# Earlier token sums, a written order for the last part's first pair and norm, and operands on multiples of 512 bytes, in a one-core trunk layer

## The chip, the cores and the metric

The kernel runs on one core of a Trainium2 chip. The metric is the device time of one execution in microseconds (us). Five engines have queues of their own: TensorE (PE, matmuls), VectorE (DVE), ScalarE (ACT), GpSimd (POOL) and SyncE (SP, which only issues transfers here; POOL issues some too).

## The reference, cut to what matters

The reference is one decoder layer for 512 tokens of width 1024. The change touches its two feed-forward parts and nothing of the mixer's arithmetic.

```python
D_MODEL, SEQ, D_FF = 1024, 512, 2816

def rmsnorm(x, g):
    y = x * lax.rsqrt(jnp.mean(x * x, axis=-1, keepdims=True) + EPS)
    return y * g

def swiglu(x, w_in, w_out):
    a, b = jnp.split(x @ w_in, 2, axis=-1)
    return (jax.nn.silu(a) * b) @ w_out

h = x + 0.5 * swiglu(rmsnorm(x, ffn1_norm), ffn1_w_in, ffn1_w_out)
h = h + hybrid_mixer(rmsnorm(h, mix_norm), w_in, ...)   # projection, HGRN2, gated delta rule, output
h = h + 0.5 * swiglu(rmsnorm(h, ffn2_norm), ffn2_w_in, ffn2_w_out)
y = rmsnorm(h, final_norm)
```

## The kernel before, in words

**Data.** Features lie on the 128 partitions and the 512 tokens along the free axis, so the stream `h` is 8 tiles of 128x512. Every float32 product is made of three matmuls: both operands are split into a high part (a rounded copy) and a low part (the rest), and high·high, high·low and low·high are summed in PSUM (`mm3`, lines 166 to 168). For the weights the names are `whi` and `wlo`, for the normalised tokens `uh` and `ul`. The stationary operand is a 128x128 piece of the weights; the tokens stream past it, 512 or 256 columns at a time.

**A feed-forward part** has two stages. The first makes `silu(a)·b` in 22 pieces of 128 hidden columns. A few pieces are computed plainly: the opening (lines 597 to 657) computes three of the first part's, and `ffn` (line 239) one of the second part's. The other 19 or 21 run by Strassen's scheme with seven products in place of eight (`product`, line 388): A11, A12 and A22 use weights as they come (`plain`, lines 343 to 361), s1 to s4 use sums of weight blocks (`sigma`, lines 362 to 386: three sums on DVE, a high part `sig` on ACT, a low part on DVE), and four of the products need sums of tokens, t1 to t4. These are made once, in place in `h` (`tokens`, lines 281 to 302): eight scalings on ACT (L284), four sums on DVE (L287 to L293) and their split in four halves, `th` on ACT (L299) and `tl` on DVE (L301). Each product is 12 matmuls of 256 columns, so a piece is 84. Its results are collected by `columns` (copies of PSUM, of which L433 is the first one of a piece) and `gate` (L465 to L473: scale by the norm, Silu, multiply into `g`). The plain pieces go through `first` (L488 to L494) instead. The second stage multiplies by the second matrix: the first four of eight output tiles are woven between the pieces (`first_half`, `down`), the rest follows in `ffn`.

**Low parts of plain weights.** `plain` writes the negative high part into the `wlo` tile on ACT (L349) and the high part into `whi` (L352); POOL then issues a transfer that adds the weights from memory to `wlo` (L358). In all other places DVE subtracts.

**What sets the order.** Within `gated` nothing is scheduled by a compiler: `Desk` (line 50) runs these functions as threads at build time with hand-set costs and lags, and the order it finds on each engine is written out (`manual_schedule`). The opening is written out by hand the same way. The rest of the program, the mixer and the second part's plain pieces and norm among it, is placed by a scheduler. Tiles come from rings: 3 `raw` buffers of 128x512 for loads, 2 `raw2` of twice the size, 6 each of `whi` and `wlo`; PSUM lanes `mm` (2 banks), `a` and `b` (2 each). A lane's `get` waits until all that held it is read.

**The norm** of a part needs the sum of squares of all tokens: `sqacc` squares each tile of `h` (ACT) and adds it to `acc` (POOL, in the opening DVE); `stats` (line 206) sums over partitions with eight tiny matmuls `pst`, takes the root on POOL (`root`, `rcol`, L225), spreads it with `pbc` matmuls and copies it to `rbc`. The products of the first stage do not need it; `gate` and `first` do.

## Time and profile before

| | us |
|---|---|
| median of 3 runs | 1649.01 (1648.87 to 1649.12) |
| the profiled execution | 1648.81 |
| its span | 1647.0 |
| PE busy in the span | 1609.5 (98%) |
| DVE, ACT, POOL busy | 1132.4, 857.9, 414.0 |
| first part: last plain matmul of the opening starts, first piece's first L433 copy | 42.67, 46.99 |
| second part: norm's `pbc` starts, first piece's first L433 copy | 1281.31, 1292.59 |

The time of an execution is its span and 1.8 us around it. All moments below are counted from the span's start. PE's busy time includes matmuls that run back to back at whatever clock they get, so a busy share of 98% does not say that they run at full rate; the views by window give the granted clock (PEclk, 1.00 is full speed) beside it. In a row of the timeline stand the start, the duration, the engine and the line, the operation, out<-in with sizes, and in brackets the idle time of the engine just before and what ended it.

### The profile page before, as it was taken

How to read it: one execution, taken by the hardware profiler on the slowest of the kernel's cores; microseconds unless marked ns; L12 is line 12 of the kernel's file. 1: busy time of each engine (PE TensorE's matmuls, PEld its weight loads, DVE VectorE, ACT ScalarE, POOL GpSimd, SP SyncE). 2: the span in 40 equal slices, each digit the busy share in tenths (PEclk: the TensorE clock that was granted, in tenths of full speed). 3: DMA queues.
4: the chain of work that ended last, by engine and by line, in shares of the span. 5: the costliest groups of instructions: out<-in, count | busy, mean ns of one | idle time of the engine just before them, and what ended most of it. 6: DMA issues, size and time to landing. Idle time of an engine off the chain costs nothing.

```text
span 1647.0 us, 30275 instructions
## 1 busy us (share of the span) xinstructions
PE 1609.5 (98%) x11178; PEld 1414.3 (86%) x11178; DVE 1132.4 (69%) x2158; ACT 857.9 (52%) x1852; POOL 414.0 (25%) x743
## 2 busy tenths in 40 slices
PE   8799999999999999999999999999999699999997
PEld 7799998888878788888888988887888699999887
DVE  5877775547677678658888888755544677778353
ACT  6666664323424335456666665554225666667232
POOL 1222210101121221253572655500001222220011
PEclk9999999999999999999999999999999799999999
DMA  5888852532312223443333333445534788883343
GB/s 179 194 185 183 186 122 80 176 115 91 93 50 72 84 72 96 126 144 103 100 100 113 92 104 121 144 146 181 185 103 154 180 186 181 184 184 87 109 137 116
DMA packets 128166, 216.53 MB, mean 131 GB/s; under 512 B 21888, under 2 KB 27776, under 8 KB 128016
## 3 DMA queue, kind: packets, MB, share of 16 engines
q1 hardware_dynamic: 110448, 182.89, 35.4%
q0 software_dynamic: 17280, 31.46, 12.7%
q8 instruction: 88, 1.44, 0.4%
q14 instruction: 62, 0.51, 0.1%
q10 hardware_dynamic: 288, 0.22, 0.0%
HBM read 197.45 MB, written 17.07 MB: 130 GB/s over the span
## 4 chain that ended last, share of the span: by engine, by line
PE 94%; issue 2%; DMA 1%; DVE 1%; ACT 1%; POOL 0%; DVEq 0%; SPq 0%; POOLq 0%
PE pmm L166 16%; PE pmm L168 16%; PE pmm L167 15%; PE pnat L166 4%; PE pfa L168 4%; PE pnat L168 4%; PE pnat L167 4%; PE pfa L166 4%; PE pfa L167 4%; PE pfy L168 2%; PE pfy L166 2%; PE pfy L167 2%; PE pfx L168 2%; PE pfx L167 2%; PE pfx L166 2%
## 5 line engine op out<-in xcount | busy, mean ns | idle before, releaser
L166 PE MATMUL pmm<-uh,whi 128*128 128x512 f32 x632 | 263.9, 418 | 5.4 <-ACT whi L623 5.4
L1766 ACT CAST whi<-raw 128x512 fp32r<-128x512 f32 x226 | 140.1, 620 | 215.7 <-PE pmm L167 156.2
L1768 DVE TENSOR_TENSOR wlo<-raw,whi 128x512 fp32r<-128x512 f32 x226 | 161.1, 715 | 126.7 <-ACT whi L1766 120.7
L168 PE MATMUL pmm<-uh,wlo 128*128 128x512 f32 x632 | 248.1, 393 | 0.0
L167 PE MATMUL pmm<-ul,whi 128*128 128x512 f32 x632 | 247.7, 392 | 0.0
L383 DVE TENSOR_TENSOR sig<-h,sig 128x1024 fp32r<-128x1024 f32 x80 | 97.7, 1221 | 76.8 <-ACT sig L381 76.7
L166 PEld LDWEIGHTS pmm<-uh,whi 128*128 128x128 f32 x632 | 119.5, 189 | 27.0 <-ACT whi L623 5.4
L166 PE MATMUL pmm<-gh,whi 128*128 128x512 f32 (+1 forms) x374 | 142.0, 380 | 0.0
L168 PE MATMUL pmm<-gh,wlo 128*128 128x512 f32 (+1 forms) x374 | 142.0, 380 | 0.0
L167 PE MATMUL pmm<-gl,whi 128*128 128x512 f32 (+1 forms) x374 | 141.9, 379 | 0.0
L168 PEld LDWEIGHTS pmm<-uh,wlo 128*128 128x128 f32 x632 | 119.0, 188 | 26.3
L167 PEld LDWEIGHTS pmm<-ul,whi 128*128 128x128 f32 x632 | 119.6, 189 | 20.4 <-DVE ul L193 0.2
L381 ACT CAST sig<-h 128x1024 fp32r<-128x1024 f32 x80 | 83.9, 1049 | 100.5 <-PE pfa L168 91.3
L204 POOL TENSOR_TENSOR acc<-acc,sqt 128x512 f32<-128x512 f32 x18 | 24.0, 1334 | 379.6 <-ACT sqt L202 294.5
L162 DVE TENSOR_TENSOR wlo<-raw,whi 128x512 fp32r<-128x512 f32 x78 | 59.2, 762 | 74.5 <-ACT whi L161 74.5
L166 PE MATMUL pnat<-whi,uh 128*128 128x256 f32 (+1 forms) x328 | 107.7, 328 | 0.0
L168 PE MATMUL pnat<-whi,ul 128*128 128x256 f32 (+1 forms) x328 | 100.6, 307 | 0.0
L167 PE MATMUL pnat<-wlo,uh 128*128 128x256 f32 (+1 forms) x328 | 100.4, 306 | 0.0
L166 PE MATMUL pfa<-th,sig 128*128 128x256 f32 x320 | 92.2, 288 | 5.0 <-ACT sig L381 5.0
L168 PE MATMUL pfa<-th,sig 128*128 128x256 f32 x320 | 92.3, 288 | 3.2 <-DVE sig L383 3.2
L358 POOL DMA_DIRECT2D wlo<-w1b x63 | 54.6, 869 | 157.5 <-ACT s L433 99.6
L161 ACT CAST whi<-raw 128x512 fp32r<-128x512 f32 x78 | 46.3, 595 | 87.5 <-PE pmm L167 81.1
(480 smaller groups left out, 4613.8 us busy)
## 6 DMA issues: line engine op xcount, KB each, us to landing
raw<-wt SPq DMA_DIRECT2D x128, 256.0 KB
raw<-w1b SPq DMA_DIRECT2D x88, 256.0 KB
raw<-w1a SPq DMA_DIRECT2D x80, 256.0 KB
raw<-wn SPq DMA_DIRECT2D x64, 256.0 KB
wlo<-w1b POOLq DMA_DIRECT2D x63, 256.0 KB, 5.3
wlo<-w1a POOLq DMA_DIRECT2D x57, 256.0 KB, 5.5
raw<-w2b SPq DMA_DIRECT2D x45, 256.0 KB
raw<-w2a SPq DMA_DIRECT2D x40, 256.0 KB
```

The lines of the kernel that those rows point to most:

```text
L161: act.copy(hi[:, :f], raw[:, :f])
L162: dve.tensor_tensor(lo[:, :f], raw[:, :f], hi[:, :f].bitcast(F32), op=ALU.subtract)
L166: pe.matmul(pt, ah, bh, start=first, stop=False, **kw)
L167: pe.matmul(pt, ah, bl, start=False, stop=False, **kw)
L168: pe.matmul(pt, al, bh, start=False, stop=last, **kw)
L204: add.tensor_tensor(acc, acc, s, op=ALU.add)
L358: pool.dma_start(lo, src_, accum_op=ALU.add)
L381: act.copy(hl[:, 0:2], s)
L383: dve.tensor_tensor(hl[:, 2:4], s, hl[:, 0:2].bitcast(F32), op=ALU.subtract)
L1766: act.copy(hi, raw)
L1768: dve.tensor_tensor(lo, raw, hi.bitcast(F32), op=ALU.subtract)
```

## The change

Five things are done.

1. **The opening** scales each token tile right after its square, makes the token sums (now eight of 128x2x256, `sums`) and their split (`high`, `low`, class `tokens`), all before the first gates. Its third plain pair is summed in the PSUM lane `b`, not in `mm`.
2. **The first pieces** of both parts get other lags in `plain`, `sigma` and `first`, and so another order.
3. **The second part's** plain piece and norm (`plain_pairs`, `norm`) become threads of the planner. The last square is added to `acc` by POOL, so that `pst` is four matmuls.
4. **Silu** is called once on one column ahead of the second part's sums, so that its table of values is loaded; the scheduler, not the planner, has placed this call.
5. **Sizes.** `msq` becomes 128x128 and all rings of the part are laid out beforehand (`room`). Before, `g`, `gh`, `gl`, `raw2`, `th`, `tl` and `sig` of the first part began 32 bytes behind a multiple of 512 in each partition, and those of the second part at multiples of 512; now all begin at multiples of 512.

```diff
-    v = pl.tile([P, 4], F32, name="msq", bufs=1)
+    v = pl.tile([P, P], F32, name="msq", bufs=1)
...
-        early, ahead = [], []
+        early, tk = [], tokens(fp)
+        fp.tile([P, P], F32, tag="msq", name="room", bufs=1)
+        for tag, n, size in (("fa", 2, 1), ("fb", 2, 1), ("s14", 2, 1), ("s23", 2, 1), ("raw2", 2, 2), ("g", KF + 2, 1), ("big", 7, 4)):
+            fp.tile([P, size * T], F32, tag=tag, name="room", bufs=n)
         if lead is not None:
-            early, ahead = opening(w1, fp)
-            early = early + ahead
+            early = opening(w1, fp, tk)
             lead()
-        else:
-            for j in range(late):
-                for n in ("fa", "fb"):
-                    early.append(fp.tile([P, T], F32, name=n, bufs=2))
-                    act.copy(early[-1], dense(w1[j, len(early) % 2 ^ 1], KD, ux))
-        g, gh = gated(w1, w2, src, after, fp, early, lead is not None)
+        g, gh = gated(w1, w2, src, after, fp, early, tk, late)
...
+class tokens:
+
+
+
+    def __init__(self, fp):
+        self.fp, self.hq = fp, h.rearrange("p (x a) t -> p x a t", x=2)
+        self.th, self.tl = [None] * 2, [None] * 2
+
+    def scale(self, kt, c0):
+        act.activation(h[:, kt], h[:, kt], AF.Copy, scale=cs[:, c0 + kt:c0 + kt + 1])
+
+    def sums(self, g):
+        a, lo, hi = slice(2 * g, 2 * g + 2), slice(0, T // 2), slice(T // 2, T)
+        b11, b12, b21, b22 = (self.hq[:, x, a, c] for x in range(2) for c in (lo, hi))
+        yield dve.tensor_tensor(b11, b11, b12, op=ALU.subtract)
+        yield dve.tensor_tensor(b12, b22, b12, op=ALU.subtract)
+        yield dve.scalar_tensor_tensor(b22, b11, -1.0, b22, op0=ALU.mult, op1=ALU.subtract)
+        yield dve.scalar_tensor_tensor(b21, b22, -1.0, b21, op0=ALU.mult, op1=ALU.subtract)
+
+    def high(self, g, x):
+        if g == 0:
+            self.th[x], self.tl[x] = (self.fp.tile([P, 4, T], F32R, tag="big", name=n, bufs=7) for n in ("th", "tl"))
+        a = slice(2 * g, 2 * g + 2)
+        act.copy(self.th[x][:, a], self.hq[:, x, a])
+
+    def low(self, g, x):
+        a = slice(2 * g, 2 * g + 2)
+        dve.tensor_tensor(self.tl[x][:, a], self.hq[:, x, a], self.th[x][:, a].bitcast(F32), op=ALU.subtract)
...
+    opened = bool(early)
+    n0 = len(early) // 2 if opened else late
+    D = Desk(raw=RB, w=WB, raw2=2, sig=3, sum=2, fa=2, fb=2, s14=2, s23=2, mm=2, a=0 if opened else 2,
+             b=0 if opened else 2)
...
-    def tokens():
-        for kt in range(KD):
-            yield A(T)
-            act.activation(h[:, kt], h[:, kt], AF.Copy, scale=cs[:, D.c0 + kt:D.c0 + kt + 1])
...
+    def sums_of_tokens():
+        if not opened:
+            act.activation(rcols[:, 4:5], ones[:, :1], AF.Silu)
+            for kt in (0, 1, 4, 5, 2, 3, 6, 7):
+                if kt == 2:
+                    yield "lag", 2.0
+                yield A(T) if kt == 7 else ("use", "ACT", 0.02)
+                tk.scale(kt, C_F2)
+            for g in range(2):
+                for step in range(4):
+                    yield V(T) if g else ("use", "DVE", 0.02)
+                    if step == 0:
+                        it = tk.sums(g)
+                    next(it)
+                D.start((0, g), splits(g))
+            yield "on", ("split", 0), ("split", 1)
+        D.fire("tokens")
+
+    def splits(g):
         for x in range(2):
...
+            yield A(2 * T)
+            tk.high(g, x)
+            yield V(2 * T)
+            tk.low(g, x)
+        D.fire(("split", g))
...
     def loader():
+        if not opened:
+            for j in range(n0):
+                for n in range(4):
+                    yield "get", "raw", 1
+                    raw = wp.tile([P, T], F32, tag="raw", name="raw", bufs=RB)
+                    yield S
+                    sp.dma_start(raw, w1[j, n // 2, :, n % 2 * T:n % 2 * T + T])
+                    D.start((-1, j, n), split_slab(("late", j, n), raw, T))
...
-        yield "lag", 3.0
+        yield "lag", 0.0 if j == n0 else 3.0
...
     def sigma(j, r2, r12, r21):
-        yield "lag", 3.0
+        yield "lag", (0.0, 8.0 if opened else 5.0, 4.0, 3.0)[min(j - n0, 3)]
...
     def first(j):
-        a, b = early[2 * j:2 * j + 2]
-        if not opened or j == 0:
-            yield from gate(j, a, b, -1.0, a)
+        if not opened:
+            yield "on", "tokens", "rbc", ("early", 4 * j + 1)
+        a = early[2 * j]
+        if opened and j == 0:
+            yield "lag", 6.0
+            yield from gate(j, a, early[1], -1.0, a)
             return
-        tag = "a" if j == 1 else "mm"
+        tags = ("a" if j == 1 else "b",) * 2 if opened else ("mm", "a")
+        yield "lag", (0.0 if j == 1 else 7.0) if opened else 6.0
...
         t = fp.tile([P, T], F32, name="fa", bufs=2)
         dve.tensor_tensor(t, a, rbc, op=ALU.mult)
-        D.put(tag)
+        D.put(tags[0])
...
+        if not opened:
+            yield "on", ("early", 4 * j + 3)
...
-        dve.scalar_tensor_tensor(g[j], b, -1.0, t, op0=ALU.mult, op1=ALU.mult)
-        D.put(tag)
+        dve.scalar_tensor_tensor(g[j], early[2 * j + 1], -1.0, t, op0=ALU.mult, op1=ALU.mult)
+        D.put(tags[1])
...
+    def plain_pairs():
+        for j in range(0 if opened else n0):
+            for n in range(4):
+                yield "on", ("late", j, n)
+                if n % 2 == 0:
+                    yield "get", "a" if n else "mm", 1
+                hi, lo = made["late", j, n]
+                for i in range(4):
+                    yield T_(.69)
+                    if n % 2 == 0 and i == 0:
+                        early.append(psc.tile([P, T], F32, tag="pa", name="pmm", bufs=LANES["a"]) if n else
+                                     psd.tile([P, T], F32, tag="mm", name="pmm"))
+                    w = slice(i * P, (i + 1) * P)
+                    mm3(early[-1], hi[:, w], lo[:, w], *ux(n % 2 * 4 + i), n % 2 == 0 and i == 0, n % 2 == 1 and i == 3)
+                D.put("w")
+                D.fire(("early", 4 * j + n))
+
+    def norm():
+        yield "lag", 6.0
+        yield T_(.95)
+        pt = psc.tile([P, T], F32, tag="pd", name="pst")
+        for i in range(NT):
+            pe.matmul(pt[:, i:i + 1], acc[:, i * P:(i + 1) * P], ones[:, :1], start=True, stop=True)
+        yield V(4)
+        v = fp.tile([P, P], F32, name="msq", bufs=1)
+        dve.tensor_scalar(v[:, :4], pt[:, :4], 1.0 / (P * KD), EPS, op0=ALU.mult, op1=ALU.add)
+        yield "use", "POOL", 1.3
+        pool.tensor_tensor(rcol, v[:, :4], mhalf[:, :4], op=ALU.pow)
+        yield "lag", 4.0
+        yield T_(.5)
+        pb = psc.tile([P, T], F32, tag="pd", name="pbc")
+        for i in range(NT):
+            pe.matmul(pb[:, i * P:(i + 1) * P], rcol[:, i:i + 1].to_broadcast([P, P]), ident, start=True, stop=True)
+        yield A(T)
+        act.copy(rbc, pb)
+        D.fire("rbc")
...
+        yield from plain_pairs()
         yield from product()
...
+    if opened:
+        D.idle.update(PE=8.0, DVE=3.0)
+    else:
+        D.start((0, 9), norm())
+    D.start((0,), sums_of_tokens())
...
+        if d == KD - 1 and (defer or late):
             act.activation(rbc, h[:, d], AF.Square)
+            if late:
+                pool.tensor_tensor(acc, acc, rbc, op=ALU.add)
             return
...
                 sqacc(kt - 1, pl, tag="s14", add=dve)
+                tk.scale(kt - 1, C_F1)
         s = sqacc(KD - 1, pl, tag="s14")
+        tk.scale(KD - 1, C_F1)
         slabs = [slab(w[2, 0][:, :512])]
+        for n in range(2):
+            for _ in tk.sums(n):
+                pass
+        tk.high(0, 0)
+        tk.high(0, 1)
         out = []
         for pt, n in zip(pts, ("fa", "fb")):
             out.append(pl.tile([P, T], F32, name=n, bufs=2))
             act.copy(out[-1], pt)
-        slabs.append(slab(w[2, 0][:, 512:]))
+        tk.high(1, 0)
+        tk.high(1, 1)
         more = []
         def half(n):
             if n % 2 == 0:
-                more.append(psd.tile([P, T], F32, tag="mm", name="pmm"))
+                more.append(psc.tile([P, T], F32, tag="pb", name="pmm", bufs=LANES["b"]))
             for i in range(4):
                 k, c = n % 2 * 4 + i, slice(i * P, (i + 1) * P)
                 mm3(more[-1], *(x[:, c] for x in slabs[n]), *ux(k), k == 0, k == KD - 1)
         def between():
+            slabs.append(slab(w[2, 0][:, 512:]))
             half(0)
+            tk.low(0, 0)
+            tk.low(0, 1)
             slabs.append(slab(w[2, 1][:, :512]))
+            tk.low(1, 0)
+            tk.low(1, 1)
         stats(pl, s, between)
         half(1)
         slabs.append(slab(w[2, 1][:, 512:]))
         half(2)
         half(3)
-    return out + pts[2:], more
+    return out + pts[2:] + more
...
-    e["nextnorm"](C_F2, e["h2"], tag="ta", bufs=TA)(d, mp)
+    e["nextnorm"](C_F2, e["h2"], late=True, tag="ta", bufs=TA)(d, mp)
```

VectorE between the opening and the first pieces, before (names: `wlo` of L162 is the low part of a slab of the third plain pair, `h` the token sums, `fa` and `g` gates):

```order
L162 TENSOR_TENSOR wlo<-raw,whi 128x512 x2
L224 TENSOR_SCALAR msq<-pst 128x4
L162 TENSOR_TENSOR wlo<-raw,whi 128x512
L465 TENSOR_TENSOR fa<-fa,rbc 128x512
L287 TENSOR_TENSOR h<-h 128x4x256
L162 TENSOR_TENSOR wlo<-raw,whi 128x512
L289 TENSOR_TENSOR h<-h 128x4x256
L291 SCALAR_TENSOR_TENSOR h<-h 128x4x256
L293 SCALAR_TENSOR_TENSOR h<-h 128x4x256
L473 SCALAR_TENSOR_TENSOR g<-fb,fa 128x512
L488 TENSOR_TENSOR fa<-pmm,rbc 128x512
L301 TENSOR_TENSOR tl<-h,th 128x1024
```

and now:

```order
L162 TENSOR_TENSOR wlo<-raw,whi 128x512
L264 TENSOR_TENSOR h<-h 128x2x256
L265 TENSOR_TENSOR h<-h 128x2x256
L266 SCALAR_TENSOR_TENSOR h<-h 128x2x256
L267 SCALAR_TENSOR_TENSOR h<-h 128x2x256
L264 TENSOR_TENSOR h<-h 128x2x256
L265 TENSOR_TENSOR h<-h 128x2x256
L266 SCALAR_TENSOR_TENSOR h<-h 128x2x256
L267 SCALAR_TENSOR_TENSOR h<-h 128x2x256
L224 TENSOR_SCALAR msq<-pst 128x4
L162 TENSOR_TENSOR wlo<-raw,whi 128x512
L277 TENSOR_TENSOR tl<-h,th 128x1024 x2
```

The sums have moved from behind the norm and the first gate to the place right behind the first slab, and the first `tl` ahead of all gates.

TensorE where the last slab of the third plain pair meets A11, the first product (`pfa`), in the changed kernel (before, all of the pair's 48 matmuls stood ahead of the first `pfa`):

```order
L166 MATMUL pmm_397<-uh_71,whi_392 128x512
L167 MATMUL pmm_397<-ul_72,whi_392 128x512
L168 MATMUL pfa_481<-uh_71,wlo_431 128x256
L166 MATMUL pfa_481<-uh_71,whi_430 128x256
L167 MATMUL pfa_481<-ul_72,whi_430 128x256
L168 MATMUL pfa_481<-uh_71,wlo_431 128x256
```

Most of A11's matmuls now run ahead of the last slab's; `whi_392` is the last slab's high part.

ScalarE where the second part begins, before (`fa` and `fb` are copies of the plain pair, `wlo` and `whi` of L349 and L352 belong to A11):

```order
L192 ACTIVATE uh<-h,cs 128x512
L202 ACTIVATE sqt<-h 128x512
L284 ACTIVATE h<-h,cs 128x512
L239 COPY fa<-pmm 128x512
L239 COPY fb<-pmm 128x512
L219 COPY rbc<-pbc 128x512
L467 ACT_TABLE_LOAD
L467 ACTIVATE fa<-fa 128x512
```

and now:

```order
L192 ACTIVATE uh<-h,cs 128x512
L674 ACTIVATE rbc<-h 128x512
L259 ACTIVATE h<-h,cs 128x512
L386 ACTIVATE wlo<-raw_14560 128x512
L273 CAST th<-h 128x1024
L389 CAST whi<-raw_14560 128x512
L386 ACTIVATE wlo<-raw 128x512
L273 CAST th<-h 128x1024
```

The weights of A11 and the token split follow the last scaling at once; the copies of the pair, which stood between, are gone, and `rbc` and the gate come later.

48 lines of the change are left out of this document (12 added, 36 removed).

## The prediction

> **What bounds the kernel now.** I read the page's busy times and its chain of waits first.
>
> ```profile
> span 1647.0 us, 30275 instructions
> PE 1609.5 (98%) x11178; PEld 1414.3 (86%) x11178; DVE 1132.4 (69%) x2158; ACT 857.9 (52%) x1852; POOL 414.0 (25%) x743
> PE 94%; issue 2%; DMA 1%; DVE 1%; ACT 1%; POOL 0%; DVEq 0%; SPq 0%; POOLq 0%
> ```
>
> The chain that ends last is PE for 94%. An edit helps only where PE stands still, runs at a low clock, or needs longer per matmul. The windows show where that is not so: PE busy, its granted clock (seventh figure) and DMA share.
>
> ```profile
> 100.00:240.00 140.00, 140.00 (x1174) 140.00 (x1173) 107.97 (x141) 92.45 (x162) 32.09 (x38) 1.00 0.77 169
> 1340.00:1480.00 140.00, 140.00 (x1169) 140.00 (x1168) 108.12 (x139) 96.08 (x168) 36.39 (x42) 1.00 0.82 184
> 1290.00:1300.00 10.00, 7.42 (x34) 6.60 (x34) 6.70 (x7) 5.31 (x9) 1.73 (x2) 0.67 0.74 123
> 1300.00:1310.00 10.00, 6.95 (x31) 6.65 (x32) 8.50 (x10) 6.01 (x9) 2.16 (x3) 0.50 0.87 255
> ```
>
> In the steady stretches of both feed-forward parts PE is full at clock 1.00. At the second part's start it is 70% busy at clock 0.67 and 0.50. The longest waits of PE around the two starts (total, times, longest; windows 0 to 62 and 1262 to 1312):
>
> ```profile
> PE pfa L166 <- ACT sig L381: 2.8, 1, 2.8
> PE pfa L166 <- DVE fa L488: 2.2, 1, 2.2
> PE pfy L167 <- DVE tl L301: 1.8, 2, 0.9
> PE pfa L168 <- DVE sig L383: 1.6, 1, 1.6
> ...
> PE pfa L166 <- ACT whi L352: 3.6, 1, 3.6
> PE pfa L168 <- DMA wlo<-w1b: 3.3, 1, 3.3
> PE pfa L166 <- ACT sig L381: 2.2, 1, 2.2
> PE pfa L168 <- DVE sig L383: 1.7, 1, 1.7
> ```
>
> Every one concerns what the change moves. But the waits (8.4 and 10.8 us) leave out what the lowered clock costs. So I measure by the beat: the first copy L433 of each piece, the first, third and fourth of either part.
>
> ```profile
> 46.99 0.37 ACT L433 COPY s<-pfa 128x256 f32<-128x256 f32 x1 [1.01 <-PE pfa L168]
> ...
> 76.75 0.35 ACT L433 COPY s<-pfa 128x256 f32<-128x256 f32 x1
> 86.78 0.35 ACT L433 COPY s<-pfa 128x256 f32<-128x256 f32 x1
> 1292.59 0.37 ACT L433 COPY s<-pfa 128x256 f32<-128x256 f32 x1 [1.10 <-PE pfa L168]
> ...
> 1324.40 0.35 ACT L433 COPY s<-pfa 128x256 f32<-128x256 f32 x1
> 1334.48 0.35 ACT L433 COPY s<-pfa 128x256 f32<-128x256 f32 x1
> ```
>
> The steady beat is 86.78 − 76.75 = 10.03 us and 1334.48 − 1324.40 = 10.08. Where the third copy could be is set by the last plain work on PE:
>
> ```profile
> 42.67 0.39 PE L168 MATMUL pmm<-uh,wlo 128*128 128x512 f32 x1
> 45.28 0.35 PE L166 MATMUL pfa<-uh,whi 128*128 128x256 f32 x1 [2.23 <-DVE fa L488]
> 1281.31 1.05 PE L217 MATMUL pbc<-sq,rcol 128*128 128x128 f32 x8
> 1286.00 0.54 PE L166 MATMUL pfa<-uh,whi 128*128 128x256 f32 x1 [3.65 <-ACT whi L352]
> ```
>
> In the first part the pair ends at 42.67 + 0.23 (the spacing of its matmuls) = 42.90. The copy follows the start of A11 by 46.99 − 45.28 = 1.71 us. Without a stall the third copy is at 42.90 + 1.71 + 2 × 10.03 = 64.67, and it is at 76.75: **12.1 us lost**. In the second part `pbc` takes until about 1282.24 (0.93 at the spacing of its eight), the third copy could be at 1282.24 + 1.71 + 20.16 = 1304.1, and is at 1324.40: **20.3 us lost**. That is what earlier operands can win.
>
> **The change part by part.** *The opening's sums.* Eight sums of 512 columns cost as much as `h<-h,raw` of that size, 0.69 to 0.72 apart:
>
> ```profile
> 52.72 0.69 DVE L371 TENSOR_TENSOR h<-h,raw 128x512 f32<-128x512 f32 x1
> 29.22 0.69 DVE L162 TENSOR_TENSOR wlo<-raw,whi 128x512 fp32r<-128x512 f32 x1 [5.72 <-ACT whi L161]
> ```
>
> 8 × 0.72 = 5.8 us fall on 5.72 us in which DVE waited anyway; the slab behind ends some 2.7 us later than before, at 32.65, and PE wants it after the `pst`, at 34.6 (half(1)). The four `tl` (4.9 us, 1.23 each by the L368 row of that size further down) then end at 37.9, before the first gate. On ACT the eight scalings and four `th` fill its idle time of 3.39 and 5.19 before 34.9. Cover for all of this is the third plain pair, 48 matmuls; without it the sums' 5.8 us would be PE's.
>
> *A11 and the first sums.* With the pair in lane `b`, A11 need not wait for `fa` (2.23 gone). Its bound is now its own low part. POOL issues that after ACT's `wlo`:
>
> ```profile
> 37.72 2.92 POOL L358 DMA_DIRECT2D wlo<-w1a  x3 [4.96 <-PE pmm L168]
> wlo<-w1a POOLq DMA_DIRECT2D x57, 256.0 KB, 5.5
> ```
>
> ACT writes it one Silu earlier, so the issue moves to about 36.8, and with 4.3 to 5.5 us to landing (the fastest I saw and the page's median) the tile is there at 41.1 to 42.3. The third matmul of A11 now stands ten 512-column matmuls before the pair's end: 42.90 − 10 × 0.23 + 2 × 0.12 = 40.8. The wait is 0.3 to 1.5, I take 0.8. Sums of weights: `sigma`'s three sums, `sig` and its low part come to 46.9 by DVE's new row; s2 wants them at 47.7. s1's may be up to 0.3 late; I take 0.2. First part: 12.1 − 1.0 = **11.1** (9.5 to 11.8).
>
> *The second part's start.* Here A11's first load waited behind the norm: its `raw2` lies where the pool of the part before had its root.
>
> ```profile
> 1269.51 0.32 SPq L586 DMA_DIRECT2D h<-h  x1
> 1277.90 0.33 SPq L316 DMA_DIRECT2D raw<-w1b  x1
> 1277.91 0.59 ACT L239 COPY fa<-pmm 128x512 f32<-128x512 f32 x1 [5.57 <-POOL rcol L225]
> ```
>
> The new order has no root ahead: SP issues at about 1269.9, 8 us sooner, and passes one spill row; that spill is read much later. ACT writes A11's parts instead of standing 5.57 us for `rcol`. POOL first adds the last square, then issues; its root comes behind two transfers, and only gates wait for it. On DVE three sums and the last `ul` follow the last tile of `h` (1269.5 + 4 × 0.72 = 1272.4), then three sums and four `tl`: + 2.2 + 4.9 (1.23 each, row below) = 1279.5, and 1280.2 with ACT's casts between. `sigma`'s three sums (2.6), `sig` and its low part (1.0, 1.2) reach 1285.2; PE comes to A11 at about 1280.5 and to s2 at 1285.8. What is left: the low part of the second plain product landing (0 to 0.4), and A12 of the next piece behind the first gate, whose Silu now stands behind a table load of 1.28 (0.75, at most 3):
>
> ```profile
> 1283.00 1.28 ACT L467 ACT_TABLE_LOAD   x1
> 1301.43 1.23 DVE L368 TENSOR_TENSOR h<-raw,raw 128x1024 f32<-128x1024 f32 x1 [1.18 <-DMA raw<-w1b]
> ```
>
> I take 1.5 in all: 20.3 − 1.5 = **18.8** (16.5 to 19.6). Four `pst` fewer at 0.22 (1275.99 to 1276.21) give **0.9**.
>
> ```profile
> 1275.99 0.36 PE L211 MATMUL pst<-ones,acc 128*128 128x1 f32 x2
> 1276.21 0.36 PE L212 MATMUL pst<-ones,sqt 128*128 128x1 f32 x2
> ```
>
> *The early Silu.* It was placed at the mixer's start, so the load before the second part's first Silu stays, and the mixer gets two more: one to Silu's table, one back near 493. Each is 1.28 us on ACT, which stood idle 2.45 and 2.16 there; PE feeds on other work. I take nothing, at most 2.6.
>
> ```profile
> 375.72 0.62 ACT L1766 CAST whi<-raw 128x512 fp32r<-128x512 f32 x1 [2.45 <-issue]
> 490.50 0.62 ACT L1766 CAST whi<-raw 128x512 fp32r<-128x512 f32 x1 [2.16 <-PE pmm L167]
> ```
>
> *Alignment.* The two parts run the same second stage, the first at 32 bytes off, the second at multiples of 512:
>
> ```profile
> 262.00:322.00 60.00, 60.00 (x259) 48.20 (x258) 25.36 (x38) 19.23 (x33) 3.93 (x3) 1.00 0.49 145
> 1520.00:1580.00 60.00, 60.00 (x267) 49.67 (x266) 28.75 (x45) 21.99 (x39) 3.58 (x3) 1.00 0.40 119
> ```
>
> 60/259 = 231.7 ns a matmul against 60/267 = 224.7; start to start I read 6.6 less. The first part has 22 × 8 × 3 = 528 of them: 528 × 6.6 ns = 3.5 us. The products go the other way, 10.08 against 10.03: 19 × 0.05 = 0.95 lost. Net **2.5** (−1 to 3.7). The Trainium skill's page "TensorE: Matmul & The Clock Gate", section "Back-to-back issue gap", gives the isolated gap as N/2.4 + 2.5 ns, 215.8 at 512, with no term for an address: by it the sum would lack these 2.5.
>
> Sum: 11.1 + 18.8 + 0.9 + 2.5 = 33.3. Against the profiled execution's 1648.81 (0.2 under the median of 1649.01): **1615.5 us**.
>
> **The rivals.** *Stalls come back at the starts (12%).* One wait of about 3 us in each, on a transfer like the 3.3 on `wlo<-w1b` above, and the clock falls as in the rows at 1290 and 1300. For it: two such waits exist, and POOL's transfers get no faster. Against: they are issued 1 to 8 us earlier. Price: 3 us and half of 10 us at clock 0.50 in each start, 2 × 8 = 16: 1631.5. The clock section of the same page of the Trainium skill ("What's actually happening") has windows of about 3.4 us; by that a wait costs 3 + 1.7, and this rival would end at 1625.
>
> *Alignment does nothing (20%).* The two windows also differ in DMA share, 0.49 against 0.40, which could make the 7 ns. Then 1618.0.
>
> *The early Silu does not do what it says (10%).* It saves no load behind the first gate, and both added ones fall on the mixer's chain: 2.6, 1618.1.
>
> *The pieces lose their beat (3%), the slower side.* DVE has 108 of 140 us and the transfers 0.77 to 0.82 in the steady rows; another phase between pieces could make one operand late in each. It decides from 33.3/36 = 0.93 us a piece (36 steady ones); at 1 us the time is 1651.5. Against: those rows leave DVE 2.3 us a piece, and the steady order on each engine is that of before.
>
> **How the numbers follow.** The forecast has 55%, with its own range 1613 to 1618. The two rivals at 1618 lie within reach, and 1611.5 is the sum with every residue at its low bound and alignment at 3.7 (33.3 + 0.7 + 0.8 + 1.2 = 36.0), less 1.3 us because the bounds come from a walk. Upwards I go to 1626, two thirds of the way to the first rival; what is left out is about 15%. A measurement of this kernel can tell 0.2% (3.3 us) from no change; only the last rival leaves the faster side: faster 95%, same 2%, slower 3%.
>
> **What would show it.** Right: the third L433 copies near 65.7 in the first part (64.67 + 1.0) and near 1291 in the second (1304.1 + 1.5 − 0.9, less 11.1 and 2.5 won ahead of it), 10.03 to 10.08 apart from there; waits for L488 and for `whi` gone from PE's list; clock 1.00 within 10 us of either start; 528 matmuls of the first part at 225 ns. Wrong: a wait over 2 us on `wlo<-w1a` or `wlo<-w1b`, a clock of 0.5 in a window behind A11, spacing of 232 ns at the new addresses, a longer mixer (from the first part's last matmul to the last square), or a beat above 10.1.

## The result, and the profile after

The change makes the kernel 1.4% faster: 1625.61 us in the median of four runs (1623.19 to 1626.77) against 1649.07 before, a ratio of 0.9856 with a 95% interval of 0.9839 to 0.9873. The forecast was 1615.5, with 1611.5 to 1626.0 as its range, so the median lies inside it by 0.4 us; 23.5 us came of the 33.3 expected. The profiled execution took 1623.19 us. The page of the changed kernel, its span, its busy times and the engines of the chain that ends last:

```profile
span 1621.4 us, 30263 instructions
PE 1599.5 (99%) x11170; PEld 1408.9 (87%) x11170; DVE 1134.0 (70%) x2166; ACT 858.5 (53%) x1853; POOL 414.6 (26%) x744
PE 92%; DMA 3%; issue 1%; ACT 1%; DVE 1%; POOL 0%; SPq 0%; DVEq 0%; ACTq 0%; POOLq 0%
```

PE is still the bound, but transfers now hold 3% of the chain, where they had 1%. The waits of PE around the two starts (total, times, longest; windows 0 to 62 and 1255 to 1300; without the 5.6 us at the beginning of the program, which were 5.4 before) are shorter and fewer than before:

```profile
PE pfa L168 <- DMA wlo<-w1a: 0.8, 1, 0.8
PE pfy L168 <- DVE sig L420: 0.6, 1, 0.6
PE pfa L168 <- DVE sig L420: 0.5, 1, 0.5
...
PE pfy L168 <- DVE sig L420: 2.9, 1, 2.9
PE pfx L166 <- DVE g L537: 0.8, 1, 0.8
```

One long wait is left, 2.9 us in the second part, on the low part of a sum of weights. The beat, by the first copy of a piece (L470 now, L433 before; the first, third and fourth piece of each part):

```profile
48.41 0.36 ACT L470 COPY s<-pfa 128x256 f32<-128x256 f32 x1
...
70.15 0.35 ACT L470 COPY s<-pfa 128x256 f32<-128x256 f32 x1
79.27 0.35 ACT L470 COPY s<-pfa 128x256 f32<-128x256 f32 x1
...
1273.07 0.35 ACT L470 COPY s<-pfa 128x256 f32<-128x256 f32 x1
...
1299.33 0.35 ACT L470 COPY s<-pfa 128x256 f32<-128x256 f32 x1
1309.41 0.35 ACT L470 COPY s<-pfa 128x256 f32<-128x256 f32 x1
```

The fourth copy of the first part came 86.78 − 79.27 = 7.5 us sooner. (It is better to go by the fourth than by the third, which I had used: matmuls of the plain pair are now mixed with the first piece's, so the copies fall into step only there.) The fourth one of the second part came 1334.48 − 1309.41 = 25.1 sooner, and the beat is 10.08 in both parts.

Three marks cut the program into parts that can be compared one by one: the fourth copy, the last tile of `h` that the first part writes (369.27 before), and the last tile of `h` that the mixer writes (1268.79 before). The last column is a second profile of the same changed kernel (below, "change again").

| term, us saved | forecast | first profile | second profile |
|---|---|---|---|
| first part's start (fourth copy, the beat's 0.15 added back) | 11.1 | 7.7 | 6.3 |
| rest of the first part: alignment | 2.5 | 2.6 | 2.6 |
| mixer, between the two `h` marks (899.5 before) | 0 | 0.1 | −3.7 |
| second part, from the mixer's last `h` to the last piece (236.9 before) | 19.7 | 14.7 | 14.6 |
| behind that | 0 | 0.5 | 0.1 |
| span | 33.3 | 25.6 | 20.0 |

So two terms are right, the alignment and the mixer (in the first profile). The two starts gave 8.4 us less than I had worked out in the first profile and 9.9 less in the second.

Where did they stay? In the first part `pst`, which ends the opening, starts 0.55 us later (at 29.79 in place of 29.24), and the gaps of PE from 41 to 80 add up to 3.4, where I had left 1.0. (A gap is here what the starts of two matmuls are apart beyond their spacing at full rate: standing still and slow matmuls together.) In the second part the gaps from 1255 to 1300 are 6.7, where I had left 1.5. Three engines show the reason. First ScalarE and SP in the first part, and VectorE, ScalarE and SP in the second:

```profile
39.93 0.33 SPq L358 DMA_DIRECT2D raw<-w1a  x1
45.38 0.63 ACT L386 ACTIVATE wlo<-raw 128x512 fp32r<-128x512 f32 x1 [3.86 <-DMA raw<-w1a]
47.48 1.03 ACT L418 CAST sig<-h 128x1024 fp32r<-128x1024 f32 x1
48.54 1.23 DVE L420 TENSOR_TENSOR sig<-h,sig 128x1024 fp32r<-128x1024 f32 x1 [0.16 <-ACT sig L418]
...
1272.12 0.33 SPq L366 DMA_DIRECT2D raw<-w1b  x1
1273.57 0.33 SPq L358 DMA_DIRECT2D raw<-w1b  x1
1278.11 1.23 DVE L405 TENSOR_TENSOR h<-raw,raw 128x1024 f32<-128x1024 f32 x1 [2.23 <-DMA raw<-w1b]
1279.25 1.22 DVE L420 TENSOR_TENSOR sig<-h,sig 128x1024 fp32r<-128x1024 f32 x1
1280.84 0.63 ACT L386 ACTIVATE wlo<-raw 128x512 fp32r<-128x512 f32 x1 [4.27 <-DMA raw<-w1b]
```

In the first part ScalarE reaches the second piece's second block, stands 3.86 us for its load (issued at 39.93, used at 45.38: 5.4 us), and `sig`, which PE needs, is queued behind it; its low part on VectorE follows at 48.54. In the second part VectorE stands 2.23 us before the sum L405 of the *next* piece, whose block was issued at 1272.12 (6.0 us), and the low part L420 that PE waits for is queued behind it. From 1280 to 1284 the granted clock is 0.57. Windows of 4 us (length, busy time and count of PE, PEld, DVE, ACT, POOL, then granted clock, DMA share, GB/s):

```profile
40.00:44.00 4.00, 3.25 (x21) 2.63 (x20) 4.00 (x6) 1.52 (x3) 1.17 (x2) 1.00 0.95 170
44.00:48.00 4.00, 4.00 (x27) 3.59 (x26) 0.95 (x3) 2.62 (x5) 0.86 (x1) 1.00 1.07 261
1276.00:1280.00 4.00, 1.63 (x12) 1.43 (x12) 1.89 (x2) 0.57 (x1) 0.00 (x0) 1.00 1.02 233
1280.00:1284.00 4.00, 3.47 (x17) 3.47 (x18) 2.29 (x5) 2.59 (x6) 1.11 (x2) 0.57 1.08 324
```

The transfer engines are full (0.95 to 1.08; the view counts a packet whole in the window in which it begins, so a share can pass 1) while VectorE is busy for 0.95 of the 4 us from 44 on, and PE for 1.63 of those from 1276 on. In the steady stretch the view of transfers (queue, packets, MB, share of the 16 engines; then issues) from 60 to 240 us says what each kind costs:

```profile
q0 software_dynamic: 7010, 12.75, 47.3%
q1 hardware_dynamic: 10093, 18.37, 29.8%
...
raw<-w1a SPq DMA_DIRECT2D x60, 256.0 KB
wlo<-w1a POOLq DMA_DIRECT2D x48, 256.0 KB, 5.4
raw<-w2a SPq DMA_DIRECT2D x9, 256.0 KB
```

POOL's adding transfers (queue q0) take 0.473 × 180 / 48 = 1.77 us of all sixteen engines each, a load 0.298 × 180 / 69 = 0.78. Three and four of them in a piece are 8.4 us, against a beat of 10.08. At a start that is to begin at the beat at once, several pieces' worth is asked for together. That is the theory the experiments test. One rival is that the order of the instructions alone is at fault; another is that the loads are issued late, because their buffers come free late.

### The profile page after: what moved, and what is told of

Read it like the earlier page. It is cut to its first block, busy times and chain, and to the rows that moved or that the text cites. A ratio compares the mean times of both kernels' runs of the same rounds, so it can differ in the third digit from the quotient of the medians.

```text
span 1621.4 us, 30263 instructions
## 1 busy us (share of the span) xinstructions
PE 1599.5 (99%) x11170; PEld 1408.9 (87%) x11170; DVE 1134.0 (70%) x2166; ACT 858.5 (53%) x1853; POOL 414.6 (26%) x744
## 4 chain that ended last, share of the span: by engine, by line
PE 92%; DMA 3%; issue 1%; ACT 1%; DVE 1%; POOL 0%; SPq 0%; DVEq 0%; ACTq 0%; POOLq 0%
PE pmm L166 16%; PE pmm L167 15%; PE pmm L168 15%; PE pnat L166 4%; PE pnat L168 4%; PE pnat L167 4%; PE pfa L166 3%; PE pfa L167 3%; PE pfa L168 3%; PE pfx L166 2%; PE pfx L168 2%; PE pfx L167 2%; PE pfy L168 2%; PE pfy L167 2%; PE pfy L166 2%
## 5 line engine op out<-in xcount | busy, mean ns | idle before, releaser
L1865 ACT CAST whi<-raw 128x512 fp32r<-128x512 f32 x226 | 140.1, 620 | 214.5 <-PE pmm L167 156.8
L1867 DVE TENSOR_TENSOR wlo<-raw,whi 128x512 fp32r<-128x512 f32 x226 | 160.6, 711 | 128.3 <-ACT whi L1865 121.8
L420 DVE TENSOR_TENSOR sig<-h,sig 128x1024 fp32r<-128x1024 f32 x80 | 97.7, 1221 | 70.4 <-ACT sig L418 70.4
L162 DVE TENSOR_TENSOR wlo<-raw,whi 128x512 fp32r<-128x512 f32 x74 | 54.9, 746 | 67.6 <-ACT whi L161 66.9
L167 PE MATMUL pfa<-tl,sig 128*128 128x256 f32 x320 | 90.7, 283 | 0.0
```

Of the source, the lines that this page charges most:

```text
L162: dve.tensor_tensor(lo[:, :f], raw[:, :f], hi[:, :f].bitcast(F32), op=ALU.subtract)
L167: pe.matmul(pt, ah, bl, start=False, stop=False, **kw)
L420: dve.tensor_tensor(hl[:, 2:4], s, hl[:, 0:2].bitcast(F32), op=ALU.subtract)
L1865: act.copy(hi, raw)
L1867: dve.tensor_tensor(lo, raw, hi.bitcast(F32), op=ALU.subtract)
```

## The experiments

All are edits of the changed kernel except "alignment alone". They ran on several chips, on which the kernel before took 1648.8 to 1649.7 us. Marks of the profiles, with the median time beside them (us; "first start" is the fourth copy, "second part" from the mixer's last `h` to the last piece):

| kernel | median | first start | mixer | second part |
|---|---|---|---|---|
| before | 1649.1 | 86.8 | 899.5 | 236.9 |
| change | 1625.6 | 79.3 | 899.4 | 222.2 |
| change again | 1627.2 | 80.6 | 903.2 | 222.3 |
| sum later | 1626.7 | 81.1 | 900.1 | 223.4 |
| load early | 1624.0 | 80.2 | 900.0 | 220.3 |
| first order | 1626.9 | 83.2 | 901.2 | 222.1 |
| alignment alone | 1646.1 | 88.2 | 898.8 | 236.1 |
| low parts on GpSimd | 1630.3 | 81.8 | 899.8 | 225.0 |
| low parts on VectorE | 1626.3 | 80.0 | 899.5 | 222.1 |
| no early Silu | 1626.7 | 81.4 | 901.2 | 221.9 |
| load early, Silu moved | 1626.7 | 81.0 | 899.9 | 223.2 |
| the same, offset 64 | 1625.2 | 83.0 | 899.8 | 221.9 |
| offset 64 (one run) | 1624.4 | 80.1 | 900.4 | 221.3 |
| offset 128 (one run) | 1628.4 | 80.4 | 899.0 | 221.4 |

Six of these profiles (the two of the change, sum later, load early, no early Silu, Silu moved) have the same instructions in the first part, and its fourth copy lies between 79.3 and 81.4. The first start is thus uncertain by 2 us from run to run, and perhaps by more: with the rings at offset 64 the same instructions gave 80.1 and 83.0. The second part has the same instructions in four kernels of the table (the two of the change, first order, no early Silu) and varies by 0.4.

### The same kernel again

Edit: none.

> The changed kernel itself, for how much its starts vary from run to run: FFN-start gaps differed by 1.3 us between runs whose first part has the same instructions (first part's fourth copy at 79.27, 81.09, 80.24). If loads at the start are served in varying order, the second profile shows other waits of TensorE than the first (first part 3.4, second part 6.7 us of gaps), and times spread over 1623 to 1627; if the first profile is typical, the same waits within 0.3 us.

1627.23 us (1624.14 to 1628.82); the profiled execution took 1628.82. The gaps of PE are 4.8 in the first part (3.4 the first time) and 6.8 in the second (6.7). The long wait in the second part is the same, now 3.45 us. The new loss of 3.8 us lies in the mixer, which the change leaves as it was but for two table loads. PE's waits there, in this profile and, behind the dots, in the first:

```profile
PE ptv L1372 <- DVE gqm L1316: 2.0, 1, 2.0
...
PE ptv L1372 <- DVE gqm L1316: 0.4, 1, 0.4
```

From 682 to 687 us the granted clock is 0.66 behind this wait. The wait is 1.6 longer than in the first profile, and (1 − 0.66) × 5 = 1.7 us go with the clock: 3.3 of the 3.8. In the other profiles of the kernels below that show this wait it lies between 0.3 and 1.1, 0.9 in the one without the early Silu, so the two table loads do not explain it. What makes it vary was not tried. For the verdicts below it means that a difference of 2 us between two medians of the changed kernel says nothing; the marks by part say more.

### The sum later, and the load earlier

The first edit lets VectorE take the next piece's sum behind both low parts:

```diff
-            yield "lag", (0.0, 8.0 if opened else 5.0, 4.0, 3.0)[min(j - n0, 3)]
+            yield "lag", (0.0, 8.0 if opened else 7.0, 4.0, 3.0)[min(j - n0, 3)]
```

> Changed kernel, but in the second part the first sum of weights of the second piece (L405) stands on VectorE behind both low parts (L420) of the piece before, not between them. TensorE's order is unchanged. Theory A (the 2.9 us wait of TensorE on the second low part, and the 2 us of half clock after it, come from VectorE standing 2.23 us at that sum for a load): the wait is gone, the gaps of TensorE between 1255 and 1300 fall from 6.7 us to 2 to 3, the time goes from 1625.6 to about 1621.5. Theory B (the transfers are at their limit there, and some operand is late whatever the order): a wait of 2 to 3 us shows up on another operand of the second piece, and the time stays within 1 us of 1625.6.

1626.74 us (1625.73 to 1628.18), and the second part is 223.4, 1.1 longer. The wait on L420 fell from 2.9 to 0.3, and another took its place. ScalarE's row that released it, and PE's waits from 1255 to 1300:

```profile
1283.36 0.63 ACT L386 ACTIVATE wlo<-raw 128x512 fp32r<-128x512 f32 x1 [4.03 <-DMA raw<-w1b]
...
PE pfa L166 <- ACT s L475: 2.7, 1, 2.7
PE pfx L166 <- DVE g L537: 1.0, 1, 1.0
PE pfy L168 <- DVE sig L420: 0.3, 1, 0.3
```

ScalarE stands 4.03 us for a block of the third piece, and the copy L475, which frees PE's bank, is queued behind it. This is theory B of the two: the order on VectorE alone is not the cause, and taking one engine out of the way of the late loads puts the next one in it.

The second edit leaves VectorE's order and takes the load of that sum out of the ring of three `raw` buffers:

```diff
-                yield "get", "raw", 1
-                r21 = wp.tile([P, T], F32, tag="raw", name="raw", bufs=RB)
+                if opened or j != n0 + 1: yield "get", "raw", 1
+                r21 = wp.tile([P, T], F32, tag="raw", ...) if opened or j != n0 + 1 else fp.tile([P, T], F32, tag="g", name="raw", bufs=KF + 2)
...
-            yield "lag", (0.0, 8.0 if opened else 5.0, 4.0, 3.0)[min(j - n0, 3)]
+            yield "lag", (0.0, 8.0 if opened else 13.0, 4.0, 3.0)[min(j - n0, 3)]
```

> Changed kernel with VectorE's, ScalarE's and TensorE's order as it is around that wait, but the fourth block of the second part's second piece is loaded into a free buffer of the g ring, so that its load does not wait for one of the three raw buffers: it is issued about 9 us earlier. Theory A (a late load in front of the low part): the sum no longer waits, the low part comes about 1.5 to 2 us sooner, TensorE's wait falls from 2.9 to under 1.2, the time to about 1622. Theory B (transfers at their limit): the sum or another one still waits over 2 us, time within 1 us of 1625.6. If the order on VectorE alone were the cause (the sum's own 1.2 us), the wait would fall by less than half and stay above 1.5.

1624.01 us (1623.17 to 1625.47), the second part 220.3, the shortest of all: 1.9 of the missing 5 came back. The sum no longer waits, and the wait on L420 is 0.6. PE's waits fall by only 0.7 us in sum (3.0 in place of 3.7), but none is as long as 2 us, and the granted clock is 1.00 from 1255 to 1300; the half clock behind the long wait had cost the change (1 − 0.57) × 4 = 1.7 us. But the next sum of VectorE stands 3.08 us for its load, and the wait for `g`, a piece later, grew from 0.8 to 1.7:

```profile
1284.12 1.22 DVE L405 TENSOR_TENSOR h<-raw,raw 128x1024 f32<-128x1024 f32 x1 [3.08 <-DMA raw<-w1b]
...
PE pfx L166 <- DVE g L537: 1.7, 1, 1.7
PE pfy L168 <- DVE sig L420: 0.6, 1, 0.6
```

So the load's lateness was the cause of the 2.9, and it is handed on to the pieces behind. The time expected for this case, about 1622, was missed by 2 us.

### ScalarE's order in the first part

```diff
-            yield "lag", 0.0 if j == n0 else 3.0
+            yield "lag", 0.0 if j == n0 else 5.0 if opened and j == n0 + 1 and n == "A12" else 3.0
```

> Changed kernel, but in the first part ScalarE makes the high and low parts of the second piece's second block behind the two Silu and the first high part of the sums, where it now stands 3.86 us ahead of them for a load. Nothing moves on the other engines. Theory A (this wait holds up the first sums): TensorE's waits of 0.5 and 0.6 on L420 go, with 0.3 of slower matmuls behind them; the fourth first copy comes 1.3 to 1.6 us sooner (79.3 to about 77.8) and the time falls by as much, to about 1624.1. Theory B (TensorE would wait for the second piece's block instead): the waits move there, and the time stays within 0.5 us.

1626.87 us (1625.70 to 1629.27), and the first start is at 83.2, 2 to 4 us later than with the order of the change (79.3 to 81.4). The planner has put the second piece's *third* block where the second one was, and that one landed later still. PE then waits 2.2 us for the copy L470, which is queued behind it on ScalarE:

```profile
39.96 0.49 SPq L361 DMA_DIRECT2D raw<-w1a  x1
48.49 0.63 ACT L386 ACTIVATE wlo<-raw 128x512 fp32r<-128x512 f32 x1 [6.89 <-DMA raw<-w1a]
...
PE pfa L166 <- ACT s L470: 2.2, 1, 2.2
```

The load took 8.5 us from issue to use. Both theories missed: the edit did not get the loads out of `sig`'s way. It shows again that what stands ahead of `sig` and of the copies on ScalarE decides, and that a load issued among adding transfers (POOL's were issued from 37.8 to 41.4) can take that long.

### Fewer adding transfers

In the first two pieces of each part the low parts are computed instead of summed by a transfer, on GpSimd in one kernel; in another, for the first piece only, on VectorE (`dve`, cost `V(T)`, `n0 + 1`):

```diff
             hi, lo = slot()
+            if j < n0 + 2:
+                act.copy(hi, raw)
+                yield "use", "POOL", 1.4
+                pool.tensor_tensor(lo, raw, hi.bitcast(F32), op=ALU.subtract)
+                made[j, n] = hi, lo
+                D.fire(("h", j, n))
+                D.fire((j, n))
+                return
             act.activation(lo, raw, AF.Copy, scale=-1.0)
```

> Changed kernel, but the low parts of the plain weights of each part's first two pieces are subtracted by GpSimd (1.3 us each by the L204 rows) in place of an adding transfer: six transfers less at each start, and ScalarE writes no negative copies there. An adding transfer takes 1.77 us of all 16 transfer engines in the steady stretch (47.3% of 180 us for 48), a load 0.78. Theory C (the loads of the second and third piece land 5 to 6 us after issue because adding transfers fill the engines; whatever engine meets them first stands): six times 1.77 = 10.6 us of transfer time go from each start, waits on raw fall under 1.5 us on ScalarE and VectorE, TensorE's gaps fall from 3.4 to 4.7 to under 1.5 in the first part and from 6.7 to 8 to under 3 in the second, time about 1619. Theory D (the loads are late because the three raw buffers are freed late; landing is no matter): the raw waits and a wait of TensorE over 2 us stay in the second part, time 1623 to 1626.

1630.30 us (1629.32 to 1632.45): 4.7 slower than the change, 3.1 slower than its 1627.23 on the same chip, where about 1619 was expected. Yet the first half of theory C holds. SP's issue of the second piece's second block, ScalarE's use of it, and the windows that the change had at a DMA share of 0.95 and 1.07:

```profile
40.15 0.33 SPq L358 DMA_DIRECT2D raw<-w1a  x1
43.26 1.25 ACT L387 CAST whi<-raw 128x512 fp32r<-128x512 f32 x2 [2.83 <-DMA raw<-w1a]
...
40.00:44.00 4.00, 4.00 (x26) 3.52 (x25) 4.00 (x5) 1.17 (x3) 4.00 (x3) 1.00 0.55 172
44.00:48.00 4.00, 4.00 (x27) 3.59 (x26) 3.73 (x5) 2.04 (x4) 4.00 (x3) 1.00 0.31 90
```

With the adding transfers gone the same load takes 3.1 us, not 5.4, and the transfer engines are 0.55 and 0.31 busy. ScalarE still stands 2.83 us, where under 1.5 was expected: the load is issued no earlier than in the change, so the late issue (theory D) has a part in the wait. What was lost is on VectorE. A pair of its low parts of tokens, in the change and in this kernel, and GpSimd's six subtractions of the first part:

```profile
1268.59 2.36 DVE L277 TENSOR_TENSOR tl<-h,th 128x1024 fp32r<-128x1024 f32 x2 [0.17 <-ACT th L273]
```

```profile
1269.54 4.55 DVE L277 TENSOR_TENSOR tl<-h,th 128x1024 fp32r<-128x1024 f32 x2
37.48 11.15 POOL L389 TENSOR_TENSOR wlo<-raw,whi 128x512 fp32r<-128x512 f32 x6 [4.22 <-ACT whi L387]
```

While GpSimd subtracts (1.86 us each, not 1.3), VectorE's pair takes 4.55 us in place of 2.36. In the second part the sums of weights end late by it, ScalarE's `sig` waits 8.3 us for them, and PE's longest wait, 3.6 us, is for a copy queued behind `sig`. The Trainium skill's page "SBUF — State Buffer", section "Who interferes with whom", says that a VectorE instruction with two inputs in SBUF and a GpSimd instruction that reads SBUF exclude each other; these rows agree with it. The root of the norm also had to queue behind four subtractions on GpSimd, which cost PE 1.5 us.

> Changed kernel, but the low parts of the first piece's plain weights in each part are subtracted by VectorE (0.69 each) in place of three adding transfers. Theory C (adding transfers delay the loads behind them): the second piece's second block, which landed 5.4 us after its issue in the first part, lands within 4; TensorE's wait on wlo for A11 goes; but VectorE has 2 us more ahead of the first sums, so 0 to 2 us less in all, 1624 to 1626. If GpSimd's slow subtracts and not the order made the run with them worse, VectorE's instructions keep their 0.69 and 1.22 here.

1626.30 us (1624.17 to 1628.00). VectorE keeps its durations (0.68 and 1.21), so it was GpSimd that slowed it. The load takes 3.0 us, and PE's wait for A11's low part is gone:

```profile
39.67 0.33 SPq L358 DMA_DIRECT2D raw<-w1a  x1
42.63 0.63 ACT L394 ACTIVATE wlo<-raw 128x512 fp32r<-128x512 f32 x1 [1.89 <-DMA raw<-w1a]
...
52.33 0.63 ACT L394 ACTIVATE wlo<-raw 128x512 fp32r<-128x512 f32 x1 [3.34 <-DMA raw<-w1a]
```

The start as a whole, 80.0, is that of the change all the same: VectorE's sums end 2.9 us later (46.95 in place of 44.05), and from the next piece on, whose low parts are transfers again, ScalarE stands for a load (3.34 us at 52.33). So these two kernels show that the adding transfers make the loads land late; that the part gets shorter when a load is in time is shown by "load early" alone, for 1.9 us.

### Alignment alone, and other offsets

In the kernel before, `msq` of 128x128 and the rings laid out beforehand (`room`), nothing else:

```diff
-        v = pl.tile([P, 4], F32, name="msq", bufs=1)
+        v = pl.tile([P, P], F32, name="msq", bufs=1)
...
             early, ahead = [], []
+            fp.tile([P, P], F32, tag="msq", name="room", bufs=1)
+            for tag, n, size in (("fa", 2, 1), ...): fp.tile([P, size * T], F32, tag=tag, name="room", bufs=n)
```

> Kernel before with the fifth step alone: msq of 128x128 and the rings laid out beforehand, so that the first part's operands start at multiples of 512 bytes. Theory (the address sets the spacing): an output tile of the first part's second stage takes 14.96 us in place of 15.40, a piece of products 10.08 in place of 10.03, in sum 3.5 less and 0.95 more: 1649.1 goes to 1646.5. Rival (the spacing came from the transfers' share or from something else in the change): 15.40 and 10.03 stay, 1649.1.

1646.08 us against 1649.69 on the same chip; the ratio is 0.9981 (0.9971 to 0.9990), which is 3.1 less (1.6 to 4.8), with 2.6 forecast. The window of the first part's second stage with this edit alone (the row of before stands in the prediction):

```profile
262.00:322.00 60.00, 60.00 (x266) 49.69 (x265) 25.49 (x39) 19.88 (x34) 3.92 (x3) 1.00 0.52 153
```

266 matmuls where there were 259, at a transfer share of 0.52 where it was 0.49: the share is not the reason. From `h` to `h` an output tile takes 14.96 us (15.40 before), a piece of products 10.08 (10.03). PE's instructions are those of before, so the address is the cause. (The first start, 88.2, is 1.4 later than before's; the longer pieces make 0.15 of it, and the rest was not tried. Runs of the change differ by 2 there.)

Two more offsets were set by `msq` of 16 and of 32 columns:

> Changed kernel with msq of 16 columns, so that in both parts all rings begin 64 bytes behind a multiple of 512 (before: 32 in the first part). If any offset from 512 costs, the output tiles of both second stages take 15.40 us and a piece of products 10.03; if 32 bytes are special and 64 are enough, 14.96 and 10.08.

> Changed kernel with the rings 128 bytes behind a multiple of 512. Pieces took 10.08, 10.03 and 9.97 us at 0, 32 and 64 bytes: if that goes on in proportion, 9.86 at 128; if only the offset within some block of 64 or 128 bytes matters, 10.08 again. Output tiles took 14.96, 15.40 and 15.11: no rule yet; within 14.9 to 15.4.

| bytes behind a multiple of 512 | piece of products, us | output tile, us |
|---|---|---|
| 0 (change) | 10.08 | 14.96 |
| 32 (first part before) | 10.03 | 15.40 |
| 64 | 9.99 | 15.11 |
| 128 | 10.05 | 15.34 |

The 9.97 of the expectation is 9.99 when it is read from copy to copy. No rule that I had written down fits. At 0, 64 and 128 both parts of the program give the same values, so they are no accident of one place; 32 was measured in the first part alone. Forty pieces and sixteen tiles make 642.6 us at 0, 641.4 at 64, 647.6 at 32 and 647.4 at 128. Which operand does it (the moving `th`, `gh`, `g` or the stationary `sig`) was not tried.

### The early Silu

```diff
-                act.activation(rcols[:, 4:5], ones[:, :1], AF.Silu)
+                pass
```

> Changed kernel without the early Silu on one column: the mixer loses two table loads, the load ahead of the second part's first Silu stays as it is. As predicted (ScalarE's idle time covers both loads): the time stays within 1 us of 1625.6. Rival (they fall on the mixer's chain): 2 to 2.6 less, 1623.

1626.69 us (1625.42 to 1628.51), beside 1627.23 for the change on the same chip: no difference, as forecast. The mixer takes 901.2, within what it takes with both loads (899.0 to 903.2).

Put where it would work, behind the second high part of the second part, and together with the early load:

```diff
-            yield "lag", (0.0 if j == 1 else 7.0) if opened else 6.0
+            yield "lag", (0.0 if j == 1 else 7.0) if opened else 1.0
+            if not opened: yield "use", "ACT", 0.1; act.activation(rcols[:, 4:5], ones[:, :1], AF.Silu); yield "lag", 4.9
```

> The kernel with the early load (second part, second piece's fourth block into a g buffer), and the early Silu moved from before the mixer to ScalarE's place behind the second high part of the second part, where ScalarE stood 1.55 us for a load. The load of the table ahead of the gate's Silu goes, and with it most of TensorE's wait of 1.71 on g (L537) seen with the early load. Theory: second part (last output tile of the mixer to last piece) 1.2 to 1.7 us shorter than with the early load alone (220.3), time from 1624.0 to about 1622.5. Rival: the wait on g is set by the sums and transfers ahead of it, the time stays at 1624.

1626.73 us (1625.12 to 1627.05); the second part is 223.2, 2.9 longer than with the early load alone. The table is loaded at 1278.89 as wanted, and PE's wait before A12 is 2.4, now for `fa` (L495) and not for `g`:

```profile
1278.89 1.28 ACT L525 ACT_TABLE_LOAD   x1
...
PE pfx L166 <- DVE fa L495: 2.4, 1, 2.4
```

VectorE's sum there (L405) stands 3.84 us for its load, and all gates are behind it, so the rival fits: the loads set that wait, not the table. But the edit has also moved the gates behind more of VectorE's work (the low part L420 now stands ahead of the pair's first gate), so the run does not separate the table from the order.

> The kernel of the run before with all rings of both feed-forward parts 64 bytes behind a multiple of 512. At that offset the changed kernel's pieces took 9.97 us in place of 10.08 and its output tiles 15.11 in place of 14.96. Theory (the address sets both): 40 pieces x 0.11 = 4.4 us less, 16 tiles x 0.15 = 2.4 more, 2.0 less in all: about 1620.5. Rival (that single profile differed for another reason): the same time as the run before.

1625.17 us (1621.38 to 1627.42), where about 1620.5 was expected. The pieces take 9.99 us again, so the address does what the single profile said; with 9.99 the forecast would have been 40 × 0.09 = 3.6 less and 2.4 more, 1.2 in all. The 1.6 us between this median and the 1626.73 of the run before lie within the spread of either. No kernel of these beats the change beyond doubt; the early load, at 1624.01, comes nearest.

## Why the prediction was right, and where it was not

**Which way, and within the range: right, the range by little.** The median is 0.4 us inside the range; 1625.6 is 10 us off the forecast of 1615.5 and outside the 1613 to 1618 that had the 55%, and the repetition gave 1627.23, just outside the range. What bounds the kernel was read rightly. The time lost at the two starts was there to be won: the waits for L488 and for `whi` of A11 are gone from PE's list, and ScalarE no longer stands for `rcol`. But the third copies came at 70.15 and 1299.33, where 65.7 and 1291 were to show the forecast right.

**The two starts: the mechanism right, the size off by 3.4 to 4.8 and by 5.0 us.** The step that failed is the walk of the new order: "`sigma`'s three sums, `sig` and its low part come to 46.9 by DVE's new row" and, for the second part, that only the landing of one low part and the table load were left. The low part was ready at 48.54 + 1.23 = 49.8. I had walked ScalarE and VectorE with durations of instructions, and let the loads of the second and third piece be in time: their waits were put at nothing. In the profile of before such a load took 2.6 us, from this issue to the sum L368 at 1301.43:

```profile
1298.83 0.33 SPq L329 DMA_DIRECT2D raw<-w1b  x1
```

Now the loads took 5.4, 6.0 and 7.3. The runs with fewer adding transfers show why, 3.0 and 3.1 us in place of 5.4, and the run with an early load shows that this was what PE waited for in the second part. No run got back more than 1.9 of the second part's 5 us, so it stays open whether loads in time would win back all of the loss. The windows of before had the warning: a transfer share of 0.77 in the steady rows leaves a start at full beat little to catch up with. A11's low part came as forecast, with a wait of 0.8, but partly by luck: it was issued at 37.41 in place of 36.8, and PE came to it about 0.6 later too.

**The rival of stalls** named the right kind of event, a transfer, a wait of about 3 us and the clock's fall behind it (0.57 from 1280 to 1284), but on the wrong transfer (`wlo`, where it was `raw`) and in both parts, where it came in the second alone. Its price was 8 us for a start. In gaps it was 5.2 (6.7 less the 1.5 foreseen), and the wait and the clock alone make 2.9 + (1 − 0.57) × 4 = 4.6. By the clock section ("What's actually happening") of the Trainium skill's page "TensorE: Matmul & The Clock Gate", which the prediction had set beside it, a wait costs 3 + 1.7 = 4.7 us; this trace agrees.

**Alignment: right**, 2.6 in the profile with 2.5 forecast, and 3.1 (1.6 to 4.8) alone. The rival that it does nothing falls. The matmuls of 512 columns took 15.40 us / 66 = 233 ns and 14.96 / 66 = 227, which differ by the address alone. The section "Back-to-back issue gap" of the same page of the Trainium skill has no term for an address.

**The early Silu: right** that it saves no load and costs nothing.

**A term I did not have** is the opening's own 0.55 us. The eight more scalings on ScalarE are not its cause: the last tile's square starts at 22.99 (21.64 before), 6.8 us ahead of `pst`, and PE waits for nothing from its first matmul to `pst` in either kernel. Its matmuls of 512 columns are about 0.43 us apart at first and 0.23 later, and the step comes at 9.5 us before and at 10.5 now. The windows from 9 to 13, before and now, with 18 and 15 matmuls on a PE that never stands:

```profile
9.00:13.00 4.00, 4.00 (x18) 3.22 (x17) 3.63 (x6) 4.00 (x8) 0.00 (x0) 1.00 0.86 273
...
9.00:13.00 4.00, 4.00 (x15) 3.19 (x15) 3.28 (x6) 3.94 (x8) 0.00 (x0) 1.00 0.91 283
```

In the other runs with the same opening that moment lies between 8.6 and 11.9 us, and `pst` starts between 28.85 and 30.54 with it. So the 0.55 varies from run to run and is not a price of the change that these runs show; the column of the granted clock does not show the slow beginning, and its cause was not tried.

## What to carry to other kernels

Making operands earlier moves a start to the next limit; before counting the stall as won, add up the transfers that the first pieces need together, by the engine time of each kind, and set that against the time from the first free buffer to the first use. On an engine that works in order, one instruction that waits for a load of the next piece holds up everything behind it, and the two reorderings tried here only passed the wait on to another instruction while the load stayed late. Lay operands out on purpose and measure two or three offsets: the address changed the time of a matmul by 3% here.

## What was not expected of the hardware

An adding transfer of 256 KB took 1.77 us of all sixteen transfer engines from 60 to 240 us, a load of the same size 0.78. GpSimd's subtraction of 128x512 took 1.86 us beside a busy VectorE, and made VectorE's take up to twice as long (4.55 against 2.36 us for two). The offset of the rings from a multiple of 512 bytes changed matmuls of 256 columns and of 512 columns in opposite ways, and not in proportion to the offset: 120.0, 119.4, 118.9 and 119.6 ns with 256 columns, 226.7, 233.3, 228.9 and 232.4 with 512, at 0, 32, 64 and 128 bytes.
